# A two-block kernel on one core: first head's queries and keys kept on chip, stores on another queue, turns one block later, masks for 256 keys

## The chip, the cores and the metric

The kernel runs on one core of a Trainium2 chip. The metric is the device time of one execution in microseconds (us); several executions are run and the median is quoted. Engines are called PE (TensorE, matmuls), ACT (ScalarE), DVE (VectorE), POOL (GpSimd) and SP (SyncE, which here only issues DMA transfers). Times in the text without another origin count from the start of the profiled span.

## The reference

The input has 1024 positions of 1024 numbers. A first block (recurrent unit, convolutions, feed-forward) is followed by a second block, in whose latter part the change lies. Cut to that part:

```
h = x @ w_in
x_q, x_kv, k_rope_raw, gate_a, u_pool, gate_b = split(h)
q = (rms_norm(x_q) @ w_uq)         # 4 heads x (128 "nope" + 64 "rope")
kv = (rms_norm(x_kv) @ w_ukv)      # 4 heads x (128 k_nope + 128 v)
q_rope, k_rope = apply_rope(q_rope), apply_rope(k_rope_raw)
s = (q_nope @ k_nope.T + q_rope @ k_rope.T) * 192 ** -0.5
mask = positions[q] >= positions[k]
o = softmax(where(mask, s, min)) @ v      # per block of 128 queries
y_a = o * silu(gate_a)
x = layer_norm(alpha * x + concat(y_a, y_b) @ w_out)
```

## The kernel before

Products are made in split float32: each operand is a rounded high part and the remainder (`split`, line 85: ACT casts the high part, DVE subtracts), and a product is three matmuls (high by high, high by low, low by high). All matmuls stand on line 95 and are told apart by the names of their tiles; transposes of the attention stand on line 1089. Tiles of 128x1024 float32 come from one pool of 35 buffers (`U`), eight-block tiles from a pool of 4 (`HT`), PSUM tiles from a pool of 4 (`PS`).

The work up to the attention is a list of *chunks*. Each has a load (DMA, issued three chunks ahead, `LEAD`), a cut (split of the weights, one chunk ahead) and a body (matmuls). Leftover work of one chunk is posted to the next. The last chunks are, in the order of the list on line 993:

- `A0 A1` and, later, `A2 A3` (`ga_chunk`): the gates `wga`, 48 matmuls each; ACT's silu, then POOL stores the gate of each head to DRAM (`GA`, line 855).
- `r0` and `r1` (`q_rope_chunk`, `q_rope_fin`, lines 877 to 908): the rope queries of heads 0 and 1, then of 2 and 3. ACT copies the product to `qra`; POOL issues four transfers of 32 rows each that swap halves into `qrb` (line 783); DVE turns (lines 787 to 789: two products and a sum), ACT and DVE split, and SP stores the parts to DRAM as `QT` of each head, two 256 KB transfers per head (lines 907, 908).
- `n0` and `n1` (`q_nope_chunk`): the other queries; two split tiles of 512 KB per head are stored by SP as `QN` (`spill`, line 999).
- `V0` (`kv_chunk`): keys (`kn`, split, stored by SP as `KN`) and values (`v`, kept on chip as `Vh`, `Vl`), alternately for the four heads. Then every engine reads a flag and branches (lines 983, 984): with positions in order, the attention of the causal form runs, else the full form. With the inputs here it is the causal one.

At chunk `A2` a hook calls `masks_make` (line 1006). SP loads the positions, copied to all 128 partitions (`pk`, 512 KB), and a small transposed copy (`qm`); DVE makes the flag (lines 1021 to 1027) and the parts of positions that the masks compare (lines 1029 to 1036, 14 instructions in all). Then, for each of 8 blocks of queries, POOL does one and DVE two instructions of 128x1024 (lines 1042 to 1044) for the mask, posted over three chunks.

The attention (line 1049) runs over 32 blocks `n` (4 heads of 8 blocks of 128 queries). Blocks 2q and 2q+1 of a head see the first 256(q+1) keys. At step `n` the program has:

- `scores(n)`: matmuls of `s` (three of `kn` by `qn`, two of `kkh`, `kkl` by `qt`, for each 512 or 256 keys); DVE adds the mask and takes the maximum (line 1071), ACT takes the exponential (line 1073); later `weights(n)` scales (reciprocal on DVE, copy on ACT, line 1079);
- `turn(n-2)`: PE transposes the weights to `t`; ACT casts to `PT` (line 1093) and DVE subtracts (line 1094);
- at even `n` from 4: `values((n-4)/2)`: `o`, the product with the values for a pair of blocks, times the gate on DVE and split to `yah`, `yal`.

`head_load` fetches `kn`, `qn`, `qt` of a head from DRAM on SP (five transfers): that of head 0 right after the branch, that of the next head at the third block of each head. The scheduler of the language sets the order of instructions on each engine; SP and POOL issue their transfers in the order of their rows. After the attention, `last_product` makes the output of each of 8 blocks of rows; three of them lie in the loop's last steps.

Of the kernel before, what the change touches and what calls it, by code (L numbers as in the profile page):

```python
# [11 lines left out]
F32R = mybir.dt.float32r  # L12
# [8 lines left out]
P = 128  # L21
S = 1024
D = 1024
NT = 8
# [31 lines left out]
def kernel(ctx: ExitStack, tc: tile.TileContext, I, out):  # L56
# [9 lines left out]
    def U(nm, dt=F32, shape=(P, 1024)):  # L66
        count[0] += 1
        return up.tile(list(shape), dt, name=f"{nm}_{count[0]}", tag="U", bufs=NU)
# [13 lines left out]
    def f(ap):  # L82
        return ap.bitcast(F32)
# [820 lines left out]
    def q_rope_fin(a, b, p):  # L904
        hi, lo = split(rotate_2(a, b), "qr")
        for j, rows_ in enumerate((LOW, HIGH)):
            SY.dma_start(QT_d[2 * p + j][LOW], f(hi)[rows_])
            SY.dma_start(QT_d[2 * p + j][HIGH], f(lo)[rows_])

    def q_nope_chunk(p):  # L910
# [12 lines left out]
        def body(items):  # L923
            for it in items:
                it()
            for j in range(2):
                ps = PS("qn")
                for n in range(2):
# [3 lines left out]
                    products(ps[:, n * 512:(n + 1) * 512], terms)  # L932
                spill(QN_d[2 * p + j], split(ps, "qn"))
            if p == 1:
# [4 lines left out]
    def kv_chunk():  # L939
# [12 lines left out]
        def body(items):  # L952
# [3 lines left out]
            def kn(h):  # L956
                ps = PS("kn")
                for n in range(2):
# [4 lines left out]
                    products(ps[:, n * 512:(n + 1) * 512], terms)  # L963
                spill(KN_d[h], split(ps, "kn"))

            VV.extend([HT("Vh"), HT("Vl")])
            for t2 in range(4):
                kn(t2)
                ps = PS("v")
# [28 lines left out]

    def spill(dst, parts):
        for d, t in zip(dst, parts):  # L1000
            SY.dma_start(d, f(t))

    masks = []
    in_order = cp.tile([1, 1], I32, name="in_order")

    def masks_make():
        pos = I["positions_2"]
# [6 lines left out]
        qf = U("qf", F32, (P, 16))  # L1014
        hq, lq = qf[:, 0:8], qf[:, 8:16]


# [9 lines left out]
        V.tensor_copy(in_order, below[:, 3:4])  # L1027
        ki = U("ki", I32)
        V.tensor_scalar(ki, pk, 12, None, ALU.arith_shift_right)
        V.tensor_scalar(hk, ki, 4096.0, None, MUL)  # L1030
        V.tensor_scalar(ki, pk, 4095, None, ALU.bitwise_and)
        V.tensor_copy(lk, ki)
        V.tensor_scalar(qi, pq, 12, None, ALU.arith_shift_right)
        V.tensor_scalar(hq, qi, -4096.0, None, MUL)
        V.tensor_scalar(qi, pq, 4095, None, ALU.bitwise_and)
        V.tensor_copy(lq, qi)

        def make(i):
            m = U("mtmp")
            if i % 2 == 0:  # L1040
                masks.append(U("mask", BF16, (P, 2, S)))
            G.tensor_scalar(m, hk, 1.0, hq[:, i:i + 1], MUL, ADD)
            V.scalar_tensor_tensor(m, lk, lq[:, i:i + 1], m, SUB, ADD)
            V.tensor_scalar(masks[i // 2][:, i % 2, :], m, 0.0, -1e30, ALU.is_gt, MUL)

        for i in range(NT):
            post(i // 3, lambda i=i: make(i))

    def attention(causal):

        N = 32

        def seen(i):
# [4 lines left out]
        def scores(n):  # L1058
# [11 lines left out]
            st = small("st", 4, 4)  # L1070
            V.tensor_tensor_reduce(s, ps[:, 0:w], masks[i // 2][:, i % 2, 0:w], 1.0, -3.0e38, ADD, MAX, st[:, 0:1])  # L1071
            V.tensor_scalar(st[:, 1:2], st[:, 0:1], -QK_SCALE, None, MUL)  # L1072
# [51 lines left out]

        head_load(0)
        gate_load(0)
        for n in range(N + 3):
            if n % 8 == 2 and n // 8 < 3:
                head_load(n // 8 + 1)
            if n % 8 == 5 and n // 8 < 3:  # L1130
                gate_load(n // 8 + 1)
            if n < N:
# [7 lines left out]
                if n % 8 == 4 and n // 8 >= 1:  # L1140
                    h = n // 8
                    for e in ([0, 1] if h == 1 else [h]):
                        wo[e] = split(wo[e], "wo2")
            if 2 <= n < N + 2:
                turn(n - 2)
            if n >= 4 and n % 2 == 0:
                values((n - 4) // 2)
            if n < N:
# [7 lines left out]
            if n >= N:  # L1156
                last_product(n - N, ya, wo, Rt, gB, bB)
        for t in range(3, NT):
            last_product(t, ya, wo, Rt, gB, bB)
# [90 lines left out]
```

## Time and profile before

| quantity | us |
|---|---|
| runs, median | 1782.55 |
| runs, lowest and highest | 1780.77, 1785.01 |
| the profiled execution | 1784.65 |
| its span in the trace | 1782.9 |
| PE busy | 1728.7 (97% of the span) |
| DVE, ACT, POOL busy | 979.2, 640.4, 138.5 |

The profile is of one execution, which took 2.1 us more than the median of the runs. Its page gives each engine's busy time, the chain of work that ended last, and groups of instructions by line; other views show stretches of time (windows), one engine's instructions in order (timeline), and what ended each idle time. In a timeline row the first number is the start, the second the duration, and a bracket at the end gives the idle time before the row and what ended it. [...]

### The profile page before, as it was taken

What the parts mean: (1) busy time and instruction counts of PE and PEld (TensorE: products, weight loads), DVE (VectorE), ACT (ScalarE), POOL (GpSimd) and SP (SyncE); (2) the same over time, 40 slices, a digit from 0 to 9 for tenths busy, and PEclk for the clock granted to TensorE, in tenths of its full rate; (3) what the DMA queues carried; (4) which work ended last, traced back from release to release, by engine and by line L of the source; (5) the groups of instructions that cost most, each with busy time, mean ns of one, the idle gap of its engine ahead of it and who ended that gap; (6) DMA issues with size and microseconds to landing.
All of it is one profiled execution on the core that took longest, in us unless ns stands there. A gap on an engine that the chain in (4) does not pass through costs nothing.

```text
span 1782.9 us, 19339 instructions
## 1 busy us (share of the span) xinstructions
PE 1728.7 (97%) x8047; PEld 1444.3 (81%) x8047; DVE 979.2 (55%) x1093; ACT 640.4 (36%) x742; POOL 138.5 (8%) x188
## 2 busy tenths in 40 slices
PE   8999999999999999999999999999999999977996
PEld 7888888888888888888888888888888888766885
DVE  7556555553745444544544534656646246384767
ACT  6777454521431311321221221222432233315761
POOL 2021111000200000000000000010200001030016
PEclk9999999999999999999999999999999999988998
DMA  6111211130111111121121110041012114626232
GB/s 205 36 42 53 59 37 48 63 100 27 50 34 59 48 44 51 47 60 36 51 59 34 60 59 27 24 139 30 24 48 60 40 38 159 199 109 259 95 119 96
DMA packets 129217, 126.04 MB, mean 71 GB/s; under 512 B 11846, under 2 KB 111140, under 8 KB 129124
## 3 DMA queue, kind: packets, MB, share of 16 engines
q1 hardware_dynamic: 126292, 116.40, 20.9%
q0 software_dynamic: 2688, 8.26, 1.3%
q8 instruction: 65, 1.06, 0.3%
q14 instruction: 28, 0.23, 0.0%
q10 hardware_dynamic: 144, 0.08, 0.0%
HBM read 101.78 MB, written 21.36 MB: 69 GB/s over the span
## 4 chain that ended last, share of the span: by engine, by line
PE 90%; DVE 4%; ACT 3%; DMA 2%; issue 1%; SPq 0%; POOL 0%; ACTq 0%; POOLq 0%
PE wf L95 29%; PE wd L95 15%; PE wo L95 7%; PE wx L95 5%; PE wg L95 5%; PE wu L95 2%; PE wgb L95 2%; PE wob L95 2%; PE xq L95 2%; PE wb L95 2%; PE ws L95 2%; PE wc L95 2%; PE o L95 2%; PE wga L95 2%; PE s L95 1%; PE xkv L95 1%
## 5 line engine op out<-in xcount | busy, mean ns | idle before, releaser
L536 DVE SCALAR_TENSOR_TENSOR ffc<-wf,fvec,ffc 128x1023 f32<-128x1023 f32 x96 | 123.0, 1282 | 302.1 <-ACT ffc L534 301.1
L534 ACT ACTIVATE ffc<-wf,fvec 128x1024 f32<-128x1024 f32 x48 | 53.6, 1116 | 378.1 <-PE wf L95 378.1
L269 DVE TENSOR_TENSOR x<-x,wd 128x1024 f32<-128x1024 f32 x96 | 116.9, 1217 | 55.3 <-PE wd L95 55.3
L269 DVE TENSOR_TENSOR x<-x,wo 128x1024 f32<-128x1024 f32 x48 | 58.4, 1217 | 57.6 <-PE wo L95 57.6
L766 POOL DMA_DIRECT2D sin_d<-angw x4 | 2.2, 549 | 679.5 <-ACT angw L757 679.5
L538 ACT ACTIVATE ffc<-ffc 128x1024 f32<-128x1024 f32 x24 | 25.5, 1061 | 58.7 <-DVE ffc L536 58.6
L95 PE MATMUL s<-kn,qn 128*128 128x512 f32 (+1 forms) x144 | 40.7, 394 | 6.0 <-DMA qn<-QN 6.0
L445 DVE SCALAR_TENSOR_TENSOR xc<-wx,vec,xc 128x1023 f32<-128x1023 f32 (+2 forms) x24 | 30.7, 1280 | 10.3 <-ACT xc L443 9.9
L95 PE MATMUL o<-PT,Vh 128*128 128x256 f32 x160 | 33.0, 298 | 2.7 <-DVE PT L1094 2.6
L95 PEld LDWEIGHTS s<-kn,qn 128*128 128x128 f32 x144 | 25.7, 207 | 10.4 <-issue 6.4
L1073 ACT ACTIVATE sc<-sc,st 128x256 f32<-128x256 f32 (+3 forms) x32 | 26.3, 823 | 21.0 <-DVE st L1072 21.0
L468 POOL TENSOR_TENSOR i<-i,xc 128x1024 f32<-128x1024 f32 x8 | 19.2, 2405 | 183.6 <-ACT i L463 183.6
L355 DVE TENSOR_TENSOR H<-T,H 128x1024 fp32r<-128x1024 f32 x24 | 29.1, 1220 | 8.0 <-ACT H L354 8.0
L317 ACT ACTIVATE xn<-x 128x1024 f32<-128x1024 f32 x24 | 25.4, 1059 | 22.5 <-DVE x L269 9.7
L1071 DVE CUSTOM_DVE_ANT_0 sc<-s,mask 128x256 f32<-128x256 f32 (+3 forms) x32 | 26.1, 821 | 12.8 <-PE s L95 12.5
L354 ACT CAST H<-T 128x1024 fp32r<-128x1024 f32 x24 | 24.2, 1011 | 23.8 <-PE T L349 23.7
L1094 DVE TENSOR_TENSOR PT<-t,PT 128x256 fp32r<-128x256 f32 (+3 forms) x32 | 26.1, 821 | 8.8 <-ACT PT L1093 8.5
L1089 PE MATMUL t<-cst,sc 128*128 128x128 f32 x160 | 23.7, 279 | 6.6 <-ACT sc L1079 6.6
L542 DVE TENSOR_TENSOR ffc<-ffc,ffc 128x1024 f32<-128x1024 f32 x24 | 29.3, 1222 | 0.5
L95 PEld LDWEIGHTS o<-PT,Vh 128*128 128x128 f32 x160 | 25.8, 194 | 4.4 <-DVE PT L1094 3.4
L476 POOL TENSOR_TENSOR i<-i,ge 128x1024 f32<-128x1024 f32 x8 | 21.3, 2657 | 101.3 <-DVE i L475 101.3
L429 ACT CAST xch<-xc 64x1024 fp32r<-64x1024 f32 x16 | 16.8, 1048 | 29.9 <-DVE xc L445 29.7
(1222 smaller groups left out, 5193.7 us busy)
## 6 DMA issues: line engine op xcount, KB each, us to landing
wf<-in_w_up_dram SPq DMA_DIRECT2D x48, 512.0 KB
wd<-in_w_down_dram SPq DMA_DIRECT2D x24, 512.0 KB
wo<-in_w_out_dram SPq DMA_DIRECT2D x16, 512.0 KB
x<-in_x_dram SPq DMA_DIRECT2D x8, 512.0 KB
wx<-in_w_in_dram SPq DMA_DIRECT2D x8, 512.0 KB
wg<-in_w_in_dram SPq DMA_DIRECT2D x8, 512.0 KB
R<-x POOLq DMA_DIRECT2D x8, 512.0 KB, 3.3
kn<-KN SPq DMA_DIRECT2D x8, 512.0 KB
```

Of the source, the lines that this page charges most:

```text
L95: PE.matmul(ps, lhsT=l, rhs=r, start=(first and j == 0), stop=(last and j == n - 1))
L269: V.tensor_tensor(X[t], X[t], ps, ADD)
L317: A.activation(xn, X[t], AF.Square, accum_out=ss[:, 0:1])
L355: V.tensor_tensor(H[1][t // 4][sl], v, f(H[0][t // 4][sl]), SUB)
L445: V.scalar_tensor_tensor(xc[:, j:], ps[:, :S - j], lw(3 - j, c), xc[:, j:], MUL, ADD)
L534: A.activation(o, ps, AF.Copy, scale=fw(2, base + fi))
L536: V.scalar_tensor_tensor(o[:, j:], ps[:, :S - j], fw(2 - j, base + fi), o[:, j:], MUL, ADD)
L538: A.activation(o, o, AF.Gelu_apprx_tanh)
L542: V.tensor_tensor(o, o, g, MUL)
L1071: V.tensor_tensor_reduce(s, ps[:, 0:w], masks[i // 2][:, i % 2, 0:w], 1.0, -3.0e38, ADD, MAX, st[:, 0:1])
L1073: A.activation(s, s, AF.Exp, scale=QK_SCALE, bias=st[:, 1:2], accum_out=st[:, 2:3])
L1094: V.tensor_tensor(lo, v, f(hi), SUB)
```

## The change

Four things are changed.

1. In `q_rope_fin` and `spill` (now `keep`) head 0's parts stay in SBUF: `QN[0]` and `KN[0]` are the split tiles themselves, `QT[0]` is a tile that two POOL transfers fill. The parts of heads 1 to 3 go to DRAM as before, but POOL issues the transfers instead of SP. The keys' order is heads 1, 2, 3, 0, and `head_load(0)` is gone; the next head's load is at step 1 of a head instead of 2.
2. The steps of the loop are 36 instead of 35: `turn(n-3)` instead of `turn(n-2)`, `values` at odd `n` from 5, and the first four `last_product` calls inside.
3. The masks of the causal form: a block's keys before its own 256 are zero (three POOL memsets of bfloat16 tiles, three mask tiles instead of four); for the own 256 keys DVE does three instructions of 128x256 (24 in all). The POOL instruction is gone.
4. The full form, which does not run here, makes its own masks in its branch.

```diff
@@ q_rope_fin
-            SY.dma_start(QT_d[2 * p + j][LOW], f(hi)[rows_])
-            SY.dma_start(QT_d[2 * p + j][HIGH], f(lo)[rows_])
+            if p == 0 and j == 0:
+                QT[0] = U("qt", F32R)
+            dst = f(QT[0]) if p == 0 and j == 0 else QT_d[2 * p + j]
+            G.dma_start(dst[LOW], f(hi)[rows_])
+            G.dma_start(dst[HIGH], f(lo)[rows_])
@@ q_nope_chunk, kv_chunk
-                spill(QN_d[2 * p + j], split(ps, "qn"))
+                keep(QN, QN_d, 2 * p + j, split(ps, "qn"))
-                spill(KN_d[h], split(ps, "kn"))
+                keep(KN, KN_d, h, split(ps, "kn"))
-                kn(t2)
+                kn((t2 + 1) % 4)
-    def spill(dst, parts):
-        for d, t in zip(dst, parts):
-            SY.dma_start(d, f(t))
+    def keep(held, dst, h, parts):
+        if h == 0:
+            held[h] = parts
+            return
+        for d, t in zip(dst[h], parts):
+            G.dma_start(d, f(t))
@@ masks
+    def mask_part(dst, parts, i, ks):
+        hk, lk, hq, lq = parts
+        m = U("mtmp")[:, ks]
+        V.tensor_scalar(m, hk[:, ks], hq[:, i:i + 1], None, ADD)
+        V.scalar_tensor_tensor(m, lk[:, ks], lq[:, i:i + 1], m, SUB, ADD)
+        V.tensor_scalar(dst, m, 0.0, -1e30, ALU.is_gt, MUL)
@@ masks_make
+        a, b, c = (U("mask", BF16, (P, 2, S)) for _ in range(3))
+        G.memset(a[:, :, 0:768], 0.0)
+        G.memset(b[:, :, 0:512], 0.0)
+        G.memset(c[:, :, 0:256], 0.0)
         def make(i):
-            m = U("mtmp")
-            if i % 2 == 0:
-                masks.append(U("mask", BF16, (P, 2, S)))
-            G.tensor_scalar(m, hk, 1.0, hq[:, i:i + 1], MUL, ADD)
-            V.scalar_tensor_tensor(m, lk, lq[:, i:i + 1], m, SUB, ADD)
-            V.tensor_scalar(masks[i // 2][:, i % 2, :], m, 0.0, -1e30, ALU.is_gt, MUL)
+            g = i // 2
+            mask_part(masks[True][i][:, g * 256:(g + 1) * 256], parts, i, slice(g * 256, (g + 1) * 256))
@@ attention
-        head_load(0)
         gate_load(0)
-        for n in range(N + 3):
-            if n % 8 == 2 and n // 8 < 3:
+        for n in range(N + 4):
+            if n % 8 == 1 and n // 8 < 3:
                 head_load(n // 8 + 1)
-            if 2 <= n < N + 2:
-                turn(n - 2)
-            if n >= 4 and n % 2 == 0:
-                values((n - 4) // 2)
+            if 3 <= n < N + 3:
+                turn(n - 3)
+            if n >= 5 and n % 2 == 1:
+                values((n - 5) // 2)
-        for t in range(3, NT):
+        for t in range(4, NT):
             last_product(t, ya, wo, Rt, gB, bB)
```

The order of instructions shows what moves. On SP before, between the load of the last gate weights and that of the positions (names: `QT`, `QN` the stores, `wkv` the weights of keys and values, `pk` the positions):

```order
L212 DMA wga_1074_9713<-in_w_in_dram 128x8x128
L946 DMA wkv_9751<-in_w_ukv_dram 128x1024
L946 DMA wkv_9753<-in_w_ukv_dram 128x1024
L907 DMA QT_120<-qrh_9762 64x1024
L908 DMA QT_120<-qrl_9763 64x1024
L907 DMA QT_121<-qrh_9762 64x1024
L908 DMA QT_121<-qrl_9763 64x1024
L1001 DMA QN_0_106<-qnh_9795 128x1024
L1001 DMA QN_1_107<-qnl_9796 128x1024
L1001 DMA QN_0_108<-qnh_9826 128x1024
L1001 DMA QN_1_109<-qnl_9827 128x1024
L1010 DMA pk_9834<-in_positions_dram 128x1024
```

On SP of the change, the same stretch, on to the attention's first transfers:

```order
L212 DMA wga_1075_9712<-in_w_in_dram 128x8x128
L949 DMA wkv_9750<-in_w_ukv_dram 128x1024
L949 DMA wkv_9752<-in_w_ukv_dram 128x1024
L1018 DMA pk_9833<-in_positions_dram 128x1024
L1021 DMA qm_9835<-in_positions_dram 128x8x1
L986 TENSOR_LOAD in_order
L987 COMPARE_AND_BRANCH
L1149 DMA ga_10153<-GA_98 128x1024
```

All eight stores between `wkv` and `pk` are gone from SP, as are the stores of the keys behind them. They stand on POOL in the change. On POOL before, around the rope transfers (`qrb`):

```order
L855 DMA GA_98<-ga_1054_9540 128x1024
L855 DMA GA_99<-ga_1059_9599 128x1024
L783 DMA qrb_9628<-qra_9627 32x1024 x4
L783 DMA qrb_9745<-qra_9744 32x1024 x4
L1042 TENSOR_SCALAR mtmp_9860<-hk_9832,qf_9838 128x1024
```

On POOL of the change, from the first rope chunk's transfers on:

```order
L783 DMA qrb_9628<-qra_9627 32x1024 x4
L910 DMA QT_119<-qrh_9643 64x1024
L910 DMA qt_9647<-qrh_9643 64x1024
L911 DMA qt_9647<-qrl_9644 64x1024
L911 DMA QT_119<-qrl_9644 64x1024
L1008 DMA QN_0_104<-qnh_9706 128x1024
L1008 DMA QN_1_105<-qnl_9707 128x1024
L783 DMA qrb_9744<-qra_9743 32x1024 x4
L910 DMA QT_120<-qrh_9761 64x1024
L911 DMA QT_120<-qrl_9762 64x1024
L910 DMA QT_121<-qrh_9761 64x1024
L911 DMA QT_121<-qrl_9762 64x1024
```

Six stores or copies now stand on POOL ahead of the second rope chunk's four `qrb` transfers; before, these four followed the first chunk's directly.

In the attention, on ACT before, around head 1's third pair of blocks (`PT_10614`; casts from `t_10615` and `t_10658`, blocks 4 and 5 of the head):

```order
L1093 CAST PT_10614<-t_10615 128x6x128
L1079 ACTIVATE sc_10584<-sc_10584,st_10585 128x768
L1073 ACTIVATE sc_10609,st_10610<-sc_10609,st_10610 128x1024
L1112 CAST yah_10564<-ga_10277 128x256
L1079 ACTIVATE sc_10609<-sc_10609,st_10610 128x1024
L1093 CAST PT_10614<-t_10658 128x6x128
```

On ACT of the change, the same pair is `PT_10621` (from `t_10622` and `t_10660`):

```order
L1125 CAST PT_10621<-t_10622 128x6x128
L1105 ACTIVATE sc_10591,st_10592<-sc_10591,st_10592 128x1024
L1111 ACTIVATE sc_10591<-sc_10591,st_10592 128x1024
L1105 ACTIVATE sc_10616,st_10617<-sc_10616,st_10617 128x1024
L1144 CAST yah_10573<-ga_10246 128x256
L1111 ACTIVATE sc_10616<-sc_10616,st_10617 128x1024
L1105 ACTIVATE sc_10655,st_10656<-sc_10655,st_10656 128x256
L1125 CAST PT_10621<-t_10660 128x6x128
```

Between the pair's two casts stand now two exponentials and two scalings of the widest blocks (1024 keys), where there was one scaling of 768 and one each of 1024. On PE the pair's second turn is followed in both kernels by one block of scores of the next head (5 matmuls of 256 keys) and the turn of block 6, and then by the pair's values.

## Rows read from the trace of the kernel before

**Rows 1.** Timeline of PE: start us, duration us, engine, line, out<-in [idle before <-releaser].

```profile
1555.16 0.61 PE L95 MATMUL wga<-H,wga3h 128*128 128x512 f32 x2
...
1571.64 0.80 PE L95 MATMUL wga<-H,wga3l 128*128 128x512 f32 x1 [15.87 <-DVE wga3l L89]
```

**Rows 2.** Timeline of DVE, same columns, around PE's first long idle time.

```profile
1544.35 1.23 DVE L787 TENSOR_TENSOR qra<-qra,cosT 128x1024 f32<-128x1024 f32 x1 [7.53 <-DMA qrb<-qra]
...
1550.28 2.35 DVE L89 TENSOR_TENSOR qnl<-qn,qnh 128x1024 fp32r<-128x1024 f32 x2
...
1563.48 0.68 DVE L1021 CAST order<-pk 1x1024 f32<-1x1024 int32 x1 [10.85 <-DMA pk<-in_positions_dram]
...
1570.38 1.21 DVE L89 TENSOR_TENSOR wga3l<-wga,wga3h 128x1024 fp32r<-128x1024 f32 x1
```

**Rows 3.** Timeline of SP's queue: transfers issued.

```profile
1536.15 1.37 SPq L212 DMA_DIRECT2D wga<-in_w_in_dram  x1
...
1549.13 0.45 SPq L907 DMA_DIRECT2D QT<-qrh  x1
...
1555.87 1.16 SPq L1001 DMA_DIRECT2D QN<-qnl  x1
```

**Rows 4.** Chain of waits, 1540 to 1625 us: start us, us, what.

```profile
1557.12 6.34 DMA pk<-in_positions_dram
...
1608.61 7.19 DMA qt<-QT
```

**Rows 5.** Windows: busy us of each engine (x instructions), PEclk, DMA share, GB/s.

```profile
1530.00:1547.00 17.00, 17.00 (x77) 14.08 (x75) 6.72 (x7) 2.95 (x4) 1.93 (x4) 1.00 1.01 290
...
1560.00:1580.00 20.00, 8.36 (x28) 6.74 (x29) 16.41 (x21) 0.00 (x0) 10.67 (x6) 0.60 0.14 33
```

**Rows 6.** Timeline of POOL, 1500 to 1600 us.

```profile
1534.90 1.93 POOL L783 DMA_DIRECT2D qrb<-qra  x4 [14.37 <-ACT qra L780]
...
1569.33 14.07 POOL L1042 TENSOR_SCALAR mtmp<-hk,qf 128x1024 f32<-128x1024 f32 x7 [32.50 <-DVE qf L1034]
```

**Rows 7.** Timeline of PE at the start of the attention.

```profile
1612.09 3.70 PE L95 MATMUL s<-kn,qn 128*128 128x256 f32 x9 [5.97 <-DMA qn<-QN]
...
1619.18 0.69 PE L1089 MATMUL t<-cst,sc 128*128 128x128 f32 x2 [1.26 <-ACT sc L1079]
...
1626.68 0.82 PE L1089 MATMUL t<-cst,sc 128*128 128x128 f32 x4 [1.89 <-ACT sc L1079]
```

**Rows 8.** Windows of heads 0 to 3, cut where a head's last values end (1727: last products).

```profile
1606.10:1650.10 44.00, 33.84 (x179) 28.25 (x179) 19.79 (x56) 23.36 (x44) 0.00 (x0) 0.81 0.65 255
1650.10:1677.95 27.85, 24.23 (x161) 21.46 (x161) 20.11 (x53) 21.43 (x40) 0.00 (x0) 1.00 0.33 114
1677.95:1703.16 25.21, 23.80 (x161) 21.42 (x161) 18.58 (x50) 20.70 (x38) 0.00 (x0) 1.00 0.14 43
1703.16:1727.00 23.84, 23.59 (x146) 20.52 (x145) 15.78 (x37) 15.70 (x27) 0.00 (x0) 1.00 0.61 221
```

**Rows 9.** Waits of PE from 1615.8 us on: us in total, times, longest.

```profile
PE t L1089 <- ACT sc L1079: 6.6, 5, 2.7
PE o L95 <- DVE PT L1094: 2.6, 3, 0.9
```

**Rows 10.** Timeline of PE at full clock: values, scores, turn.

```profile
1649.56 0.40 PE L95 MATMUL o<-PT,Vh 128*128 128x256 f32 x2
...
1649.92 0.86 PE L95 MATMUL s<-kn,qn 128*128 128x512 f32 x3
...
1651.08 0.38 PE L1089 MATMUL t<-cst,sc 128*128 128x128 f32 x2
```

**Rows 11.** ACT groups by form in head 2 (1677.95 to 1703.16): busy us, mean ns.

```profile
L1079 ACT ACTIVATE sc<-sc,st 128x1024 f32<-128x1024 f32 x2 | 2.3, 1148 | 0.0
...
L1073 ACT ACTIVATE sc<-sc,st 128x1024 f32<-128x1024 f32 x2 | 2.3, 1146 | 0.3 <-DVE st L1072 0.3
...
L1112 ACT CAST yah<-ga 128x256 fp32r<-128x256 f32 x4 | 1.6, 398 | 1.6 <-DVE ga L1111 1.6
...
L1093 ACT CAST PT<-t 128x768 fp32r<-128x768 f32 x2 | 1.6, 790 | 0.1
...
L1073 ACT ACTIVATE sc<-sc,st 128x256 f32<-128x256 f32 x2 | 1.0, 494 | 0.0
```

**Rows 12.** DVE groups by form, same stretch.

```profile
L1094 DVE TENSOR_TENSOR PT<-t,PT 128x768 fp32r<-128x768 f32 x2 | 1.9, 953 | 0.2 <-ACT PT L1093 0.2
```

More of the change, by code (lines that the diff above doesn't have):

```diff
@@ L996, with position_parts @@
             hooks[id(chunks[-1])] = [lambda: masks_make()]
-    def spill(dst, parts):
-        for d, t in zip(dst, parts):
-            SY.dma_start(d, f(t))
-    masks = []
+    def keep(held, dst, h, parts):
[4 more added lines that the diff above has]
+            G.dma_start(d, f(t))
+    masks = {}
     in_order = cp.tile([1, 1], I32, name="in_order")
-    def masks_make():
+    def position_parts():
         pos = I["positions_2"]
@@ L1015, in masks_make @@
         hq, lq = qf[:, 0:8], qf[:, 8:16]
+        ki = U("ki", I32)
+        V.tensor_scalar(ki, pk, 12, None, ALU.arith_shift_right)
+        V.tensor_scalar(hk, ki, 4096.0, None, MUL)
+        V.tensor_scalar(ki, pk, 4095, None, ALU.bitwise_and)
+        V.tensor_copy(lk, ki)
+        V.tensor_scalar(qi, pq, 12, None, ALU.arith_shift_right)
+        V.tensor_scalar(hq, qi, -4096.0, None, MUL)
+        V.tensor_scalar(qi, pq, 4095, None, ALU.bitwise_and)
+        V.tensor_copy(lq, qi)
+        return pk, (hk, lk, hq, lq)
+    def mask_part(dst, parts, i, ks):
[4 more added lines that the diff above has]
+        V.tensor_scalar(dst, m, 0.0, -1e30, ALU.is_gt, MUL)
+    def masks_make():
+        pk, parts = position_parts()
         rounded = U("order")[0:1, :]
@@ L1027, in masks_make, with masks_all @@
         V.tensor_copy(in_order, below[:, 3:4])
[L1028 to L1036, printed above, removed]
-        def make(i):
-            m = U("mtmp")
-            if i % 2 == 0:
-                masks.append(U("mask", BF16, (P, 2, S)))
-            G.tensor_scalar(m, hk, 1.0, hq[:, i:i + 1], MUL, ADD)
-            V.scalar_tensor_tensor(m, lk, lq[:, i:i + 1], m, SUB, ADD)
-            V.tensor_scalar(masks[i // 2][:, i % 2, :], m, 0.0, -1e30, ALU.is_gt, MUL)
+        a, b, c = (U("mask", BF16, (P, 2, S)) for _ in range(3))
+        G.memset(a[:, :, 0:768], 0.0)
+        G.memset(b[:, :, 0:512], 0.0)
+        G.memset(c[:, :, 0:256], 0.0)
+        own = [b[:, :, 768:1024], c[:, :, 0:512], b[:, :, 0:768], a]
+        masks[True] = [own[i // 2][:, i % 2] for i in range(NT)]
+        def make(i):
+            g = i // 2
+            mask_part(masks[True][i][:, g * 256:(g + 1) * 256], parts, i, slice(g * 256, (g + 1) * 256))
         for i in range(NT):
             post(i // 3, lambda i=i: make(i))
+    def masks_all():
+        _, parts = position_parts()
+        pairs = [U("mask", BF16, (P, 2, S)) for _ in range(4)]
+        masks[False] = [pairs[i // 2][:, i % 2] for i in range(NT)]
+        for i in range(NT):
+            mask_part(masks[False][i], parts, i, slice(0, S))
     def attention(causal):
         N = 32
+        if not causal:
+            masks_all()
         def seen(i):
@@ L1070, in scores @@
             st = small("st", 4, 4)
-            V.tensor_tensor_reduce(s, ps[:, 0:w], masks[i // 2][:, i % 2, 0:w], 1.0, -3.0e38, ADD, MAX, st[:, 0:1])
+            V.tensor_tensor_reduce(s, ps[:, 0:w], masks[causal][i][:, 0:w], 1.0, -3.0e38, ADD, MAX, st[:, 0:1])
             V.tensor_scalar(st[:, 1:2], st[:, 0:1], -QK_SCALE, None, MUL)
```

## The prediction

> **What bounds the kernel now.** I read the windows first, then PE's timeline, then who ends PE's idle times, and last the queue behind that. PE is busy 97% of the span, so only the stretches where it is not, or where its clock is down, can give much. Around the change there are two, and then small waits in the attention.
>
> The first stall: PE's row ends at 1555.77 and it starts again at 1571.64, after 15.87 us, released by DVE's `wga3l` [rows 1]. The reader should look at what DVE did before: it too was idle, 10.85 us, until the positions `pk` had landed; then came its 14 instructions for flag and positions, 1563.48 to 1570.38, 6.90 us, and `wga3l`, 1.21 us [rows 2]. The chain puts `pk`'s transfer at 1557.12, 6.34 us long [rows 4]. It was issued that late because SP's queue runs in order: the stores of `QT` and `QN` stood ahead from 1549.13 to after 1555.87 [rows 3], and these wait for data that DVE and ACT make; the weights of `wga3l` itself were issued at 1536.15 and are not the late part [rows 3]. DVE's own row at 1544.35 had waited 7.53 us for the second `qrb` [rows 2], issued by POOL at 1534.90 [rows 6], while the DMA engines were full: share 1.01, 290 GB/s [rows 5].
>
> The second stall: the first score starts at 1612.09 after 5.97 us of waiting for `qn`; `qt` lands only 7.19 us after 1608.61 [rows 4, 7]. Two turns wait for ACT, 1.26 and 1.89 us [rows 7]. Head 0 takes 44.0 us at a mean clock of 0.81, head 1 takes 27.85 and head 2 25.21, both at 1.00 [rows 8]. In the attention PE waits for weights before turns (6.6 us in 5 waits) and for the turned weights before values (2.6 in 3) [rows 9].
>
> **Part A, stores off SP's queue.** With no store ahead, `pk` waits on SP for buffers alone, and DVE's position work can follow `qnl` directly. The bound is then DVE's second rope row, at T: from 1544.35 to the end of `qnl`, 1550.28 + 2.35 = 1552.63, is 8.28 us; plus 6.90 and 1.21 gives T + 16.39 for the end of `wga3l` [rows 2]. With T as now PE would wait until 1560.7, a stall of 5.0 instead of 15.87. But six transfers, 2 MB, now stand ahead of `qrb` on POOL's queue. Late bound: 2 MB and the 0.5 MB of `qrb` through half of 290 GB/s from 1530 on [rows 5] is 17 to 18 us, T = 1548, a stall of 8.6. Early bound: `wga3l` is ready before PE is, stall 0. The 1 MB of head 0's `QN` that is not moved speaks for an early T, the shared queue for a late one; I take T = 1546, between now and the late bound: stall 6.7, **9.2 us saved**, with ends 7.2 and 15.9. The clock of this stretch is 0.60 [rows 5]; an idle time of 6.7 us may still lower it, so I take nothing for it; a full clock would give at most half of the 8.36 busy us.
>
> The trace shows that `pk` was late by its place in a queue, not by its 6.34 us of transfer [rows 3, 4]. [...]
>
> **Part B, head 0 on chip.** The wait of 5.97 and that for `qt` go. A head's work is 23.80 us of busy PE (head 2) [rows 8]. A further matmul adds 0.12 us at 256 columns and 0.23 at 512, a 128-wide turn 0.11 [rows 10]. Head 0 also does the scores of blocks 8 to 11 (5 matmuls each: 0.6, 0.6, 1.15, 1.15) before its last values, and a short turn: 27.5 us. Add fill waits, 0 to today's 1.26 + 1.89 = 3.15 [rows 7], of which I keep all; 3.6 of waits at the values (part C); and clock. Today 33.84 busy us were spent where 26.4 would do (block 11 is not in them), so the lower clock costs 7.5 us [rows 8]; with no 6 us hole at the start most of it should go, I keep 2.0, bounds 0 and 7.5. That is 36.2 instead of 44.0, and block 11's 1.15 comes off head 1: **8.9 us saved**, ends 3.4 and 14.
>
> **Part C, turns one block later.** The weights of a block have one more block of scores as cover, so the waits before turns, 6.6 us, go [rows 9]. What is late next is the turned weights. Between the two casts of the third pair ACT now has two exponentials and two scalings of 1024, a gate cast, and one exponential of 256: with both casts and DVE's subtraction 2 x 0.79 + 2 x 1.146 + 2 x 1.148 + 0.398 + 0.494 + 0.953 = 8.0 us [rows 11, 12]. PE has from the end of the pair's first turn: values of the pair before 12 x 0.12, scores 0.6, turn 6 x 0.11, scores 0.6, turn 8 x 0.11 = 4.2 us. So PE would wait up to 3.8 us there; the least is today's longest wait of this kind, 0.9 [rows 9]. I take 2.7, since ACT's first pieces may run ahead of the turn, and 0.9 for the fourth pair: 3.6 a head. Today heads 1 to 3 lose 27.85 - 24.23, 25.21 - 23.80 and 23.84 - 23.59, together 5.3 [rows 8]; then 10.8: **5.5 us lost**, with ends 0 and 9.
>
> **What counts nothing.** The mask work (POOL's 14.07 for seven [rows 6], DVE's beside it) lies at 1569 to 1596 under gate and key matmuls, and PE runs without a wait from 1571.64 until the attention; if the cover went (A larger than taken), the new 24 DVE instructions are a quarter as wide. The six key stores on POOL lie under the same matmuls; they must have landed by head 1's loads, a head later. The memsets have no row; they run on POOL, which is idle then, and only the first maximum waits for them. The extra loop step and the moved last product fall at the end, where PE has the last products anyway.
>
> Sum: -9.2 - 8.9 + 5.5 = -12.6 us. Against the profiled execution's 1784.65 that is 1772.0; it stands 2.1 above the median of the runs, 1782.55, so a median of **1770** follows.
>
> **Rivals.**
> 1. *Both holes close and no new wait comes.* Stall 1 gone (-15.9), head 0 in 27.5 (-17.6), today's waits gone (-5.3): -38.8, 1743.7. For it: all named causes are removed. Against it: ACT is busy 21.43 of 27.85 us in head 1 [rows 8], so it stays close behind PE. 0.06.
> 2. *`qrb` late behind the stores.* If POOL's transfers go out in order and slowly, T is 1553 and stall 1 is 13.7: -2.2 - 8.9 + 5.5, 1777. For it: the 7.53 us DVE already waited with four transfers alone on that queue [rows 2]. Against it: SP no longer moves the 3 MB of `QT` and `QN` then, and 1 MB of them is not moved at all. 0.15. [...]
> 3. *The change doesn't do what it says:* transfers, not the queue, bound stall 1, and `pk` lands as late. A is 0: 1779. 0.06.
> 4. *Slower.* Values wait for the turned weights at every pair, not only at the wide ones. Without waits at values the sum is -9.2 - 12.5 - 5.3 = -27.0; 16 pairs turn it over at 1.7 us each. At 2.7 each it is +16.2, 1799. For it: ACT's order puts later blocks' work ahead of the cast. Against it: narrow blocks cost ACT half, and today's waits of this kind are 0.9 at most [rows 9]. 0.05.
>
> **How the numbers follow.** My forecast, stall 1 mostly closed, first head early, values waiting at wide pairs, has 0.68. Its own ends, with the bounds partly balancing, are 1760 and 1779. I lower the low end to 1758 for a share of rival 1 and raise the high end to 1780 for rivals 2 and 3. A measurement of this kernel can tell 0.2%, 3.6 us: faster means below 1779.0. Rivals 1 and 2 and most of the forecast lie there, 0.87; the forecast's worst end and rival 3 give 0.08 the same; rival 4 gives 0.05.
>
> **What would show it.** Right: `pk` lands before 1550 and DVE goes from `qnl` to the position work with no idle row; PE's first hole is 5 to 9 us; the first score starts within 1 us of the last value product; turn waits vanish, and PE's waits before `o` on DVE's `PT` grow to about 14 us. Wrong: a hole above 12 us with DVE waiting longer for `qrb`; head 0 above 40 us; or waits before `o` above 27 us, which would make it slower.

## The result and the profile after

| | median us | lowest, highest | ratio to before, 95% interval |
|---|---|---|---|
| before | 1783.3 | 1780.77, 1785.01 | |
| the change | 1771.39 | 1770.12, 1772.31 | 0.9934 [0.9917, 0.9951] |

The change is faster by 11.9 us; a saving of 12.6, to 1770, was forecast. (A fourth run moved the median of the kernel before from 1782.55 to 1783.3.) The profiled execution's span fell from 1782.9 to 1768.3 us, by 14.6, which is more than the medians show: the profiled execution before took 1.4 us more than its median, that of the change 1.3 us less. The 14.6 us divide so, by the stretches of the prediction:

| stretch | before, us | after, us | forecast |
|---|---|---|---|
| PE's first stall | 15.87 | 6.55 | 6.7 |
| last value product of the keys' chunk ends | 1606.1 | 1596.1 | 9.2 earlier |
| head 0 | 44.0 | 34.74 | 36.2 |
| from there to the last matmul | 117.8 | 122.9 | 4.3 more (5.5, less block 11's 1.15) |

PE's timeline of the change at the first stall, where [rows 1] had 15.87:

```profile
1562.23 0.79 PE L95 MATMUL wga<-H,wga3l 128*128 128x512 f32 x1 [6.55 <-DVE wga3l L89]
```

DVE's timeline of the change, to be read against [rows 2]:

```profile
1543.07 1.23 DVE L787 TENSOR_TENSOR qra<-qra,cosT 128x1024 f32<-128x1024 f32 x1 [6.29 <-DMA qrb<-qra]
...
1548.95 2.35 DVE L89 TENSOR_TENSOR qnl<-qn,qnh 128x1024 fp32r<-128x1024 f32 x2
...
1551.21 0.77 DVE L1025 TENSOR_SCALAR ki<-pk 128x1024 int32<-128x1024 int32 x1
...
1552.75 3.90 DVE L1027 TENSOR_SCALAR ki<-pk 128x1024 int32<-128x1024 int32 x1
...
1556.68 0.69 DVE L1028 CAST lk<-ki 128x1024 f32<-128x1024 int32 x1
...
1560.95 1.23 DVE L89 TENSOR_TENSOR wga3l<-wga,wga3h 128x1024 fp32r<-128x1024 f32 x1
```

The positions are no longer waited for: their first instruction, L1025, follows `qnl` at once. SP issues them early, as its timeline shows:

```profile
1536.81 0.33 SPq L1018 DMA_DIRECT2D pk<-in_positions_dram  x1
```

But L1027, the same shape and kind of instruction as L1025, takes 3.90 us instead of 0.77. It ends at 1556.65, 0.56 us after the last memset of the masks on POOL's timeline (1555.55 + 0.54 = 1556.09):

```profile
1552.83 0.53 POOL L1008 DMA_DIRECT2D QN<-qnl  x1
1553.35 1.40 POOL L1059 MEMSET mask<- 128x1536 bf16 x1
1554.66 0.97 POOL L1060 MEMSET mask<- 128x1024 bf16 x1
1555.55 0.54 POOL L1061 MEMSET mask<- 128x512 bf16 x1
```

In the attention, the windows of heads 0 to 2 and of the rest, against [rows 8] (same columns; PEclk is the clock granted to PE, as a share of full speed):

```profile
1596.12:1630.86 34.74, 28.96 (x184) 24.49 (x182) 21.22 (x64) 25.86 (x50) 0.00 (x0) 1.00 0.37 140
1630.86:1661.45 30.59, 26.16 (x162) 23.04 (x161) 19.62 (x50) 22.04 (x39) 0.00 (x0) 0.94 0.28 104
1661.45:1689.88 28.43, 24.20 (x162) 21.50 (x161) 18.54 (x49) 20.30 (x37) 0.00 (x0) 1.00 0.13 38
1689.88:1753.80 63.92, 63.69 (x332) 53.93 (x330) 46.97 (x108) 26.35 (x39) 26.52 (x12) 1.00 0.35 124
```

The first score now starts with the end of the keys' chunk, head 0 is 9.3 us shorter, and heads 1 and 2 are 2.7 and 3.2 us longer. PE's waits from 1555 us on show why, against [rows 9]: less before turns (`t`), much before values (`o`).

```profile
PE o L95 <- ACT PT L1125: 6.0, 4, 2.6
PE o L95 <- DVE PT L1126: 3.6, 7, 0.9
PE t L1121 <- ACT sc L1111: 3.0, 3, 1.7
PE o L95 <- DVE st L1104: 1.0, 2, 0.9
```

The longest, 2.59 us, is at head 1's third pair, the place that the prediction worked out, and it was not all that was lost there: in the 5.6 us from its end the clock was 0.70, and 1.00 in the 10 us after, so that the whole head's mean is the 0.94 above.

```profile
1649.40 0.39 PE L95 MATMUL o<-PT,Vh 128*128 128x256 f32 x1 [2.59 <-ACT PT L1125]
```

```profile
1649.40:1655.00 5.60, 4.99 (x23) 4.57 (x24) 3.31 (x8) 2.45 (x6) 0.00 (x0) 0.70 0.12 50
1655.00:1665.00 10.00, 9.12 (x62) 8.13 (x61) 5.98 (x17) 6.60 (x13) 0.00 (x0) 1.00 0.01 2
```

### The profile page after: what moved, and what is told of

Same layout as the page of the kernel before. It is cut to its first block, busy times and chain, and to the rows that moved or that the text cites. A ratio compares the mean times of both kernels' runs of the same rounds, so it can differ in the third digit from the quotient of the medians.

```text
span 1768.3 us, 19326 instructions
## 1 busy us (share of the span) xinstructions
PE 1724.8 (98%) x8047; PEld 1441.5 (82%) x8047; DVE 967.2 (55%) x1101; ACT 642.4 (36%) x742; POOL 136.4 (8%) x203
## 3 DMA queue, kind: packets, MB, share of 16 engines
q1 hardware_dynamic: 122628, 103.29, 19.1%
## 4 chain that ended last, share of the span: by engine, by line
PE 91%; DVE 5%; ACT 2%; issue 1%; DMA 1%; POOL 0%; SPq 0%; DVEq 0%; POOLq 0%; ACTq 0%
PE wf L95 30%; PE wd L95 15%; PE wo L95 7%; PE wx L95 5%; PE wg L95 5%; PE o L95 3%; PE wu L95 2%; PE wgb L95 2%; PE wob L95 2%; PE xq L95 2%; PE wb L95 2%; PE ws L95 2%; PE wc L95 2%; PE wga L95 2%; PE xkv L95 1%; PE s L95 1%
## 5 line engine op out<-in xcount | busy, mean ns | idle before, releaser
L95 PE MATMUL o<-PT,Vh 128*128 128x256 f32 x160 | 34.5, 303 | 10.6 <-ACT PT L1125 6.0
L95 PEld LDWEIGHTS o<-PT,Vh 128*128 128x128 f32 x160 | 26.5, 197 | 13.7 <-ACT PT L1125 6.9
L1105 ACT ACTIVATE sc<-sc,st 128x256 f32<-128x256 f32 (+3 forms) x32 | 26.4, 825 | 14.4 <-DVE st L1104 14.3
L95 PE MATMUL s<-kn,qn 128*128 128x512 f32 (+1 forms) x108 | 28.1, 368 | 0.0
L1111 ACT ACTIVATE sc<-sc,st 128x256 f32<-128x256 f32 (+3 forms) x32 | 26.4, 828 | 2.7 <-DVE st L1110 2.0
L430 DVE TENSOR_TENSOR xch<-xc,xch 64x1024 fp32r<-64x1024 f32 x16 | 23.7, 1482 | 6.2 <-ACT xch L429 5.9
```

The source lines that it names most:

```text
L95: PE.matmul(ps, lhsT=l, rhs=r, start=(first and j == 0), stop=(last and j == n - 1))
L1105: A.activation(s, s, AF.Exp, scale=QK_SCALE, bias=st[:, 1:2], accum_out=st[:, 2:3])
L1111: A.activation(s, s, AF.Copy, scale=st[:, 3:4])
```

## The experiments

Times are medians. Each kernel was timed beside the kernel before on its chip, whose median was 1783.6 to 1783.9 there. Ratios are to that kernel; where two of their intervals overlap, the difference of the two kernels is not settled by the times.

### Which queue the stores stand on

Undone alone, in the change (a conditional keeps head 0's two copies on POOL):

```diff
-            G.dma_start(dst[LOW], f(hi)[rows_])
-            G.dma_start(dst[HIGH], f(lo)[rows_])
+            E = G if p == 0 and j == 0 else SY
+            E.dma_start(dst[LOW], f(hi)[rows_])
+            E.dma_start(dst[HIGH], f(lo)[rows_])
@@ keep
-            G.dma_start(d, f(t))
+            SY.dma_start(d, f(t))
```

> The changed kernel, with the stores of heads 1 to 3 issued by SP again; head 0 stays on chip. Theory: the positions stand behind the stores again, DVE waits for them after qnl, and the first stall is 12 to 15 us instead of 6.55: slower than the change by 6 to 9 us, about 1778 to 1780; first head and the rest as in the change. Rival (keeping head 0 on chip, which takes 1 MB and two transfers per tile off the queue, is what closed the stall): the stall stays near 6.5 us and the time within 2 us of the change's 1771.

Measured: 1782.03, ratio 0.9991 [0.9981, 1.0001]: 10.6 us slower than the change. The stall is back whole, on the positions. Its DVE and PE timelines:

```profile
1563.16 0.69 DVE L1026 TENSOR_SCALAR ki<-pk 128x1024 int32<-128x1024 int32 x1 [10.94 <-DMA pk<-in_positions_dram]
```

```profile
1570.54 0.80 PE L95 MATMUL wga<-H,wga3l 128*128 128x512 f32 x1 [15.93 <-DVE ends L1056]
```

The loss was expected to be 6 to 9; the rival, head 0 on chip as the cause, fell. More than the 9.4 us of the stall is lost because head 0 takes 36.25 us here, at clock 0.95, against 34.74 in the change:

```profile
1605.75:1642.00 36.25, 30.46 (x184) 26.02 (x183) 21.22 (x64) 25.95 (x50) 0.00 (x0) 0.95 0.48 189
```

The run also speaks against full DMA engines as the cause of the stall. Their share in 1530 to 1547, 1.01 before [rows 5] and 0.78 in the change, is as low here (0.81 in 1529 to 1546, since this run's rows stand 1.1 us earlier), and the stall is there all the same:

```profile
1530.00:1547.00 17.00, 17.00 (x77) 14.08 (x76) 6.03 (x6) 1.96 (x2) 4.67 (x7) 1.00 0.75 226
```

The other direction is the kernel before with the positions alone loaded earlier (the two loads of `masks_make` become `position_load`, called by a hook at `r1`; the rest of it stays at `A2`):

```diff
+        if w == "r1":
+            hooks[id(chunks[-1])] = [lambda: held_pos.append(position_load())]
```

> The kernel before, with one thing changed: the load of the positions is issued two chunks earlier, so that it stands on SP's queue behind the last gate weights and ahead of the eight stores of the second rope and query chunks. Theory (the positions were late by their place in SP's queue): DVE goes from the end of qnl to the position work without the 10.85 us of waiting, and PE's first stall falls from 15.87 to 5 to 7 us: faster by 9 to 11 us, about 1773. Rival (the transfers themselves are the bound, all 16 DMA engines being full): the load only pushes qrb and the weights back by its own length, the stall stays above 12 us, and the time is within 4 us of before.

Measured: 1778.73 (1774.18 to 1781.84), ratio 0.9973 [0.9962, 0.9984]; a gain of 5 us, not 9 to 11. At the place of the old stall PE waits 3.53 us, as the theory has it. But a new wait came ahead: the scheduler put an instruction on `qm` early on DVE, and `qm` now lands late, so that `wga2l` behind it made PE wait 5.1 us. DVE's timeline of this run:

```profile
1547.54 0.17 DVE L1041 TENSOR_SCALAR qm<-qm 128x8 int32<-128x8 int32 x1 [15.90 <-DMA qm<-in_positions_dram]
...
1553.56 1.23 DVE L89 TENSOR_TENSOR qrl<-qra,qrh 128x1024 fp32r<-128x1024 f32 x1 [1.16 <-ACT qrh L88]
```

So the place in the queue held the positions up, and the load moved in SP's old queue collides with other things. What the stores cost on SP in the change is shown by the first of the two runs: some 10 us.

### Head 0 through DRAM

Undone alone, in the change:

```diff
-            if p == 0 and j == 0:
-                QT[0] = U("qt", F32R)
-            dst = f(QT[0]) if p == 0 and j == 0 else QT_d[2 * p + j]
+            dst = QT_d[2 * p + j]
@@ keep
-        if h == 0:
-            held[h] = parts
-            return
@@ attention
+        head_load(0)
         gate_load(0)
```

> The changed kernel, with head 0's queries and keys stored by POOL and loaded again by SP at the start of the attention, as for the other heads (keys still in the order 1, 2, 3, 0, so that head 0's keys are the last stored). Theory (part B): PE waits for the last keys' store and load at the start, 6 to 10 us, and its clock falls in that hole; slower than the change by 8 to 13 us, about 1780 to 1784. Rival (the start waits for the softmax chain of the first blocks anyway): the transfers hide and the time is within 3 us of the change.

Measured: 1781.8, ratio 0.9990 [0.9980, 0.9999]: 10.4 us slower than the change. PE waits 6.82 us for `qn` before the first score. That is not all: head 0's `QN`, 1 MB more on POOL's queue ahead of `qrb`, delays DVE's second rope row from 1543.07 to 1546.42, and the first stall is 9.97 us instead of 6.55. DVE's timeline of this run:

```profile
1546.42 1.23 DVE L787 TENSOR_TENSOR qra<-qra,cosT 128x1024 f32<-128x1024 f32 x1 [9.70 <-DMA qrb<-qra]
...
1556.16 3.90 DVE L1022 TENSOR_SCALAR ki<-pk 128x1024 int32<-128x1024 int32 x1
```

```profile
1556.75 1.40 POOL L1054 MEMSET mask<- 128x1536 bf16 x1
1558.07 0.97 POOL L1055 MEMSET mask<- 128x1024 bf16 x1
1558.96 0.54 POOL L1056 MEMSET mask<- 128x512 bf16 x1
```

So 1 MB more of stores delays `qrb` by 3.35 us. Whether it does so by standing ahead of `qrb` on POOL's queue or by its bytes on the DMA engines this run does not part. Against the place in the queue speaks the run with the stores on SP: only 0.5 MB stand ahead of `qrb` on POOL there, and its four transfers took 6.3 to 8.6 us from issue to landing, against 6.0 to 6.4 in the change with 2 MB ahead; DVE waited 8.29 us for `qrb` in that run and 6.29 in the change. In the other direction, head 0 on chip alone, in the kernel before, with the edits of `q_rope_fin`, `keep` and the keys' order from the change but SP as issuer:

```diff
-                spill(QN_d[2 * p + j], split(ps, "qn"))
+                keep(QN, QN_d, 2 * p + j, split(ps, "qn"))
-                kn(t2)
+                kn((t2 + 1) % 4)
-        head_load(0)
```

> The kernel before, with head 0's queries and keys kept on chip as in the change (keys in the order 1, 2, 3, 0) and nothing else: stores of heads 1 to 3 on SP, turns and masks as before. Theory (part B is a gain by itself, of the wait for the transfers and of the clock after it): PE's 5.97 us hole before the first score goes, the first stall stays at 14 to 16 us; faster than before by 7 to 10 us, 1774 to 1777. Rival (the gain needs the later turns, which cover the first softmax chains): waits of 3 us or more come before the first turns, the clock still falls, and the gain is under 4 us.

Measured: 1783.35, ratio 0.9999 [0.9990, 1.0009]: no gain, against the theory. Yet head 0 itself is 10.5 us shorter than in [rows 8]; it is head 2 that takes it back. Windows of heads 0 to 2, and a row of PE's timeline in head 2:

```profile
1607.53:1641.05 33.52, 28.25 (x179) 24.78 (x178) 20.00 (x56) 23.64 (x44) 0.00 (x0) 0.95 0.46 187
1641.05:1668.93 27.88, 24.24 (x162) 21.49 (x161) 20.11 (x53) 21.43 (x40) 0.00 (x0) 1.00 0.37 133
1668.93:1701.70 32.77, 26.86 (x163) 23.96 (x162) 18.57 (x50) 20.59 (x38) 0.00 (x0) 0.90 0.10 33
```

```profile
1686.81 1.51 PE L1095 MATMUL t<-cst,sc 128*128 128x128 f32 x6 [3.85 <-ACT sc L1085]
```

Head 2 takes 7.6 us more than before, with a 3.85 us wait before a turn for ACT and the clock down to 0.90 in its mean; the first stall is 17.5 instead of 15.87. The rival had the waits before the first turns (2.09 and 2.27 us there) but not this place. The scheduler laid out head 2's rows differently, though the code for that head is the same. On ACT the first 768-wide cast to `PT` stands ahead of the first 768-wide exponential here, in the kernel before behind it (1687.62 behind 1686.68), and the exponential then waits 3.47 us for DVE:

```profile
1678.54 0.80 ACT L1099 CAST PT<-t 128x768 fp32r<-128x768 f32 x1 [1.72 <-PE t L1095]
...
1684.57 0.93 ACT L1079 ACTIVATE sc<-sc,st 128x768 f32<-128x768 f32 x1 [3.47 <-DVE st L1078]
```

That turns two blocks behind leave no room for such an order is an inference; the run with head 0 on chip and later turns, and nothing else, was not made.

### The turns

Undone alone, in the change:

```diff
-        for n in range(N + 4):
+        for n in range(N + 3):
-            if 3 <= n < N + 3:
-                turn(n - 3)
-            if n >= 5 and n % 2 == 1:
-                values((n - 5) // 2)
+            if 2 <= n < N + 2:
+                turn(n - 2)
+            if n >= 4 and n % 2 == 0:
+                values((n - 4) // 2)
@@ after the loop
-        for t in range(4, NT):
+        for t in range(3, NT):
```

> The changed kernel, with the turns of the weights two blocks behind the scores as in the kernel before, and the values in the even steps. Theory (part C: the later turns trade small waits before turns for larger waits before values, 11.5 us before o in the change): heads 1 and 2 take 27 to 28 and 25 to 26 us again instead of 30.6 and 28.4, and the kernel is faster than the change by 2 to 5 us, 1766 to 1769. Rival (the waits come from ACT being as loaded as PE, whichever instruction stands first): the waits move back from o to t with the same sum, and the time is within 2 us of the change; or the later turns did help the first head, and the kernel is slower by 2 us or more.

Measured: 1769.54, ratio 0.9926 [0.9909, 0.9943]: 1.9 us faster than the change, with overlapping intervals. The same edit the other way round in the kernel before:

> The kernel before, with nothing changed but the turns three blocks behind the scores and the values in the odd steps, as in the change. Theory (the later turns alone trade waits before t for waits before o): the 6.6 us before t shrink to under 2, the 2.6 us before o grow to 7 to 10, and the kernel is within 2 us of before or slower by up to 5. Rival (the later turns are a gain by themselves, which the first head's early start hid): faster than before by 2 us or more.

Measured: 1786.27, ratio 1.0018 [1.0009, 1.0028], 2.7 us slower. The second says that the later turns cost, the first points the same way without settling it, and both are at 2 to 3 us, less than the 5.5 forecast: in the run with earlier turns 7.8 us of waits stand before `t` again and head 2 takes 30.6 us. What the prediction took for the cause, too little distance from a pair's second turn to its values, was tried by itself:

```diff
-        for n in range(N + 4):
+        for n in range(N + 5):
-            if n >= 5 and n % 2 == 1:
-                values((n - 5) // 2)
+            if n >= 6 and n % 2 == 0:
+                values((n - 6) // 2)
@@ after the loop
-        for t in range(4, NT):
+        for t in range(5, NT):
```

> The changed kernel, with the values of a pair one block later still: 37 steps, values at even n from 6, so that two blocks of scores lie between the pair's second turn and its values instead of one. Theory (the change's waits before o, 11.5 us, come from ACT and DVE reaching the pair's second cast 1 to 3 us after PE is ready for it, while over a head ACT has idle time): most of these waits go, heads 1 and 2 take 26 to 28 us each instead of 30.6 and 28.4, and the kernel is faster than the change by 4 to 9 us, 1762 to 1767. Rival (ACT is the bound of a head, so that a later use only moves the wait): the waits come back before t or s, and the time is within 2 us of the change.

Measured: 1757.7, ratio 0.9858 [0.9841, 0.9874]: 13.7 us faster than the change, more than expected. Windows of heads 0 to 2:

```profile
1596.08:1630.00 33.92, 30.31 (x195) 26.18 (x194) 22.37 (x68) 27.58 (x52) 0.00 (x0) 1.00 0.37 143
1630.00:1655.80 25.80, 23.69 (x163) 21.33 (x162) 17.96 (x50) 21.17 (x39) 0.00 (x0) 1.00 0.34 124
1655.80:1679.80 24.00, 23.45 (x163) 21.32 (x162) 19.29 (x51) 19.90 (x39) 0.00 (x0) 1.00 0.14 45
```

Heads 1 and 2 are 4.8 and 4.4 us shorter than in the change, and the clock is 1.00 in all three, with no hole above 1.21 us. From the first score to the last matmul PE takes 145.56 us against 157.68 in the change: 8.0 us less of waits and 4.1 less of busy time. The rival, ACT as the bound, fell: ACT is as busy as before, 21.17 of 25.80 us, and no longer in the way.

### The memsets and the position work

The memsets posted two chunks later:

```diff
-        G.memset(a[:, :, 0:768], 0.0)
-        G.memset(b[:, :, 0:512], 0.0)
-        G.memset(c[:, :, 0:256], 0.0)
+        def zeros():
+            G.memset(a[:, :, 0:768], 0.0)
+            G.memset(b[:, :, 0:512], 0.0)
+            G.memset(c[:, :, 0:256], 0.0)
+        post(2, zeros)
```

> The changed kernel, with its three memsets of the masks posted two chunks later on POOL, where PE has matmuls that need nothing of DVE. In the change one DVE instruction of the position work took 3.90 us where its twin took 0.77, and it ends when POOL's memsets end. Theory (the memset holds DVE's instruction up): that instruction takes 0.7 us again, wga3l comes 3.2 us earlier, the first stall is 3.3 us instead of 6.55: faster than the change by 3 us, about 1768. Rival (the instruction waited for something else, a transfer or a semaphore): it stays at 3.9 us wherever the memsets are, and the time is the change's.

Measured: 1768.9, ratio 0.9925 [0.9909, 0.9942], 2.5 us faster than the change, with overlapping intervals, so that the trace has to settle it. The edit did half of what it should: the scheduler moved one memset and left two. DVE's and POOL's timelines:

```profile
1552.95 2.58 DVE L1027 TENSOR_SCALAR ki<-pk 128x1024 int32<-128x1024 int32 x1
...
1558.16 1.20 DVE L1053 TENSOR_REDUCE ends<-order 1x4 f32<-1x1024 f32 x1
...
1559.29 1.20 DVE L89 TENSOR_TENSOR wga3l<-wga,wga3h 128x1024 fp32r<-128x1024 f32 x1
```

```profile
1553.55 0.97 POOL L1062 MEMSET mask<- 128x1024 bf16 x1
...
1554.44 0.54 POOL L1063 MEMSET mask<- 128x512 bf16 x1
...
1558.30 1.38 POOL L1061 MEMSET mask<- 128x1536 bf16 x1 [3.32 <-DVE qf L1032]
```

L1027 is 1.32 us shorter, for a memset of 1.40 less beside it, and ends 0.55 us after the last one, as in the change. The stall is 5.14 instead of 6.55. A wait for a transfer or a semaphore would hardly become shorter by the length of a memset that was moved away. (In the run with head 0 through DRAM the 3.90 us moved with the memsets, by 3.4 us, which says less: both stand behind `qnl`.) The masks alone, in the kernel before, as the change has them:

> The kernel before, with nothing changed but the masks: zeros by three POOL memsets, DVE's 24 instructions of 128x256, no mask instruction on POOL. Theory (the masks lie under gate and key matmuls, and here POOL's memsets run before the late positions come, so that they hold no DVE instruction up): within 3 us of before, first stall 15 to 16 us. Rival (the mask work of the kernel before, POOL's 14 us beside DVE, held up the splits that the keys wait for): faster by 3 us or more.

Measured: 1783.94, ratio 1.0006 [0.9996, 1.0015]: no difference, with a first stall of 16.26 us against 15.87. Last, the position work out of the way (loads at `r1`, as above, `masks_make` at `n1`, masks and memsets posted so that they stay where they were or later; shown in part):

```diff
-        if w == "A2":
-            hooks[id(chunks[-1])] = [lambda: masks_make()]
+        if w == "r1":
+            hooks[id(chunks[-1])] = [lambda: held_pos.append(position_load())]
+        if w == "n1":
+            hooks.setdefault(id(chunks[-1]), []).append(lambda: masks_make())
@@ masks_make
+        post(3, zeros)
-            post(i // 3, lambda i=i: make(i))
+            post(1 + i // 3, lambda i=i: make(i))
```

> The changed kernel, with the positions loaded three chunks earlier and DVE's position work done while DVE waits for the second qrb; masks and their memsets where they were or later. Theory: after qnl only wga3l, 1.2 us, is left, which ends at about 1552.7, before PE is through with the first two thirds of that gate; the first stall goes (6.55 us, and its clock loss of up to 2 us): faster than the change by 6 to 8 us, 1763 to 1765. Rival (the earlier position work or its 512 KB push back the second qrb, wga2l or the weights of the second queries): PE waits 3 us or more somewhere in 1530 to 1550 instead, and the gain is under 4 us.

Measured: 1762.2 (1760.44 to 1765.28), ratio 0.9884 [0.9867, 0.9900], 9.2 us faster than the change by the medians and 7.5 by the spans of the profiled executions; 6 to 8 were expected. There is no first stall; PE waits 0.84 us once, for `wqnl`.

### Both gains together

> The changed kernel with both of the edits that gained: position work done while DVE waits for the second qrb, and values a block later still. Theory (the two act in different stretches): the gains add up, no first stall and 6 to 8 us of waits in the attention, 1747 to 1751. Rival (without the first stall the keys' work runs with less slack, and the start of the attention waits more): above 1753.

> The same with the turns two blocks behind the scores, as in the kernel before, and the values in odd steps from 5, so that also two blocks of scores lie between a pair's second turn and its values. Theory (what matters is the distance from the turn to the values, and a turn two blocks behind waits for ACT): waits before o as few as in the run with values a block later, but 5 us or more before t: 1752 to 1756. Rival (the earlier turn gives ACT its casts earlier and needs no more): within 2 us of the other version or faster.

Measured: 1748.53 (1748.26 to 1749.07), ratio 0.9806 [0.9789, 0.9822], and 1758.1, ratio 0.9861 [0.9843, 0.9879]. The first adds the gains up and beats both kernels, the change by 22.9 us. The second is slower than the 1752 to 1756 expected: PE's waits before `o` are gone, but 12.8 us stand before `t`. Both distances are needed, from scores to turn and from turn to values. PE's waits of the two, from 1510 us on:

```profile
PE o L95 <- DVE PT L1137: 2.8, 3, 1.2
PE o L95 <- DVE st L1114: 1.5, 2, 0.9
PE t L1132 <- ACT sc L1122: 1.3, 2, 0.9
```

```profile
PE t L1132 <- ACT sc L1122: 12.8, 9, 3.0
PE qn L95 <- DVE wqnl L89: 0.3, 1, 0.3
```

## Why the prediction was right, and where not

- *Bounds.* Two holes and small waits: right. The change closed 9.3 of the first hole's 15.87 us and the whole of the second, and undoing either part alone loses some 10 us.
- *Part A, 9.2 us forecast.* Right in size: the keys' chunk ends 10.0 us earlier, of which the stall gives 9.3; shown by the run with the stores on SP. But its two steps were wrong in opposite directions. "I take T = 1546" was 2.9 us too late: it is 1543.07 with 2 MB ahead of `qrb`, and 1546.42 with 3 MB. And the chain from T to the end of `wga3l` was not 16.39 us but 1560.95 + 1.23 - 1543.07 = 19.1, since L1027 took 3.1 us more than its twin. With that chain and T = 1546 the stall would have come out at 9.4; with the right T and the old chain, at 3.8. That the stall was forecast to 0.2 us is luck.
- *What counts nothing: "The memsets have no row; they run on POOL, which is idle then, and only the first maximum waits for them."* This step failed. They cost 3.1 us on PE's path (3.90 against 0.77), not by being waited for but by holding DVE up; taking one of them away gave 1.4 us of the stall back.
- *Part B, 8.9 forecast, 7.8 of it in head 0.* Head 0 fell by 9.3. Right, a little small: of the 2.0 us kept for a lower clock nothing was lost, it was 1.00. Its undoing shows a 6.82 us hole and 3.4 us by `qrb`. That it gains nothing alone in the kernel before was not foreseen; the prediction added the parts as if they were independent.
- *Part C, 5.5 lost.* Heads 1 and 2 lost 6.0 and the rest gained 0.8 (63.92 from head 2's end to the last matmul, against 64.7), so 5.2 by the windows, or 6.3 with block 11's 1.15. These do not come off head 1, as the prediction has it, since head 1 does a block of head 2 in their place (161 matmuls before, 162 in the change), but behind head 2 (336 and 332). The waits before values and their place (2.59 us at the third pair, 2.7 taken) are right. But the sum is made otherwise: behind head 0 PE's idle time grew by 3.6 us only (5.31 to 8.89), and its busy time, for less work, by 1.6 (112.49 to 114.05), most of it in head 1 (24.23 to 26.16) where the clock fell. For the clock the term had nothing. By undoing it alone only 1.9 comes back, by adding it alone 2.7 is lost, because the early turns have holes of their own.
- *Rivals.* `qrb` late behind the stores did not come: it was waited for until 1543.07, against 1544.35 before, though 1 MB more of stores, in the run with head 0 through DRAM, cost 3.35 us. Transfers as the bound fell: the move of the queue alone is worth some 10 us in the change, and with the stores on SP the stall is whole (15.93 us) at a share of the DMA engines as low as the change's (0.75 against 0.78 in 1530 to 1547). The queue's order was the bound. The slower case did not come: values waited 10.6 us in all, where 27 would have been needed.

That the prediction's total was within 1.4 us owes something to the two errors of part A balancing, 2.9 us one way and 2.7 the other. The next head's load, one step earlier in the change, was not tried by itself; in heads 1 to 3 PE waits for no transfer in either kernel.

## What to carry to other kernels

Undo a change part by part before believing its sum: here two parts are worth 10.6 and 10.4 us each when undone, one costs 2, and together they gave 12. When a transfer is late, read the issuing queue first: here SP issued the load of the positions at 1557.12 behind eight stores that waited for late data, and at 1536.81 without them. When a consumer is pipelined over blocks, look at both distances (producer to middle step, middle step to consumer): one block more in the second was worth 13.7 us. A longer first cost 2 to 3 us while the second was short, and was worth 9.6 once the second was long (1758.1 against 1748.53).

## What the runs showed of the hardware

An engine that was idle was not free to use here. DVE's 128x1024 integer instruction took 3.90 us with three POOL memsets beside it, 2.58 with two, and 0.67 to 0.78 with none. It ended 0.56 us after the last memset in the change (1556.65 and 1556.09) and in the run with head 0 through DRAM (1560.06 and 1559.50), and 0.55 us after it in the run with the later memsets (1555.53 and 1554.98). Two `TENSOR_SCALAR` of 128x256 float32 took 1.44 us together from 1558.83 in the run with the early position work, against 0.61 elsewhere; in the run with both gains, whose rows stand 0.2 us earlier there, the last two memsets ran from 1558.21 to 1559.64. A reduction of 1.20 us in the run with the later memsets (L1053 at 1558.16, memset 1558.30 to 1559.68) and two `TENSOR_TENSOR` of 2.35 together beside the first memset of the run with both gains (`wkvl` at 1556.34, memset 1556.33 to 1557.74) were not longer than elsewhere, so it is not all DVE work that is held up. What it is that holds the integer instruction no run shows. By the trace of the change it had started before the first memset (1552.75 against 1553.35) and still ended only behind the third; whether the transfer that POOL issued at 1552.83 has a part in that was not tried.

In head 1 of the change holes of 2.59 and 0.61 us in PE's work were followed by a stretch at clock 0.70 (1649.40 to 1655.00), and the 18 matmuls for the values took 4.5 us from the end of the first hole, against 3.3 for the same number in head 0, at full clock, behind holes of 1.46 and 0.61 us. The length of a hole alone does not settle it. In head 1 of the kernel before, a hole of 2.69 us left the clock at 1.00 [rows 8]. Nor does their sum: in head 0 PE was idle for 5.79 us at a clock of 0.95 in the run with the stores on SP, and for 5.78 us at 1.00 in the change. PE's timelines of the kernel before and of the change:

```profile
1655.89 0.66 PE L1089 MATMUL t<-cst,sc 128*128 128x128 f32 x4 [2.69 <-ACT sc L1079]
```

```profile
1620.33 0.39 PE L95 MATMUL o<-PT,Vh 128*128 128x256 f32 x1 [1.46 <-ACT PT L1125]
```

In the two runs with the values a block later the clock was 1.00 in each of the first three heads; the longest hole there, in the run with both gains, is 1.21 us. What decides between such cases no run here shows.
